# A hybrid encoder trunk on one core: four 512-frame blocks by seven products, the 32 new rows apart in fp32 column groups, a raw weight tile in another ring, loads ahead of frame pieces

## The chip, the cores and the metric

The kernel runs on one core of one Trainium2 chip. The metric is the device time of one execution in microseconds (us).

## The reference, cut to what matters

2048 frames of a new stream (x_prompt) and 32 frames of a running one (x_sample) pass one layer. Everything is fp32. Cut:

```python
def layer(h, p, conv_hist, pool_hist, pos, g_mix, w_in, conv_w, conv_b, pool_w, pool_scale,
          w_out, g_ple, w_ple_gate, w_ple):
    hn = rmsnorm(h, g_mix)
    proj = hn @ w_in                                # 1024 -> 6 kinds of 512
    hA, bA, cA, zA, vB, zB = jnp.split(proj, ...)
    yA, new_conv = short_conv_mixer(hA, bA, cA, zA, conv_hist, conv_w, conv_b)   # b*conv3(c*h)*silu(za)
    yB, new_pool = pooling_mixer(vB, zB, pool_hist, pos, pool_w, pool_scale)     # windows 2/4/8/16
    h = h + jnp.concatenate([yA, yB], axis=-1) @ w_out
    gate = jax.nn.sigmoid(rmsnorm(h, g_ple) @ w_ple_gate)
    h = h + (p @ w_ple) * gate
    return h, new_conv, new_pool
# then a last rmsnorm; the last 2 conv inputs and 15 pooling inputs of each stream are returned too
```

## The kernel before

Every large product is made of fp32r matmuls. An operand is split into a high part (a cast on ScalarE, `copy`) and a low part (a difference on VectorE), `split` (L79); three matmuls, high x high, high x low and low x high, stand for one (`FINE`, L160). Two blocks of frames and two halves of the depth make a 2 x 2 block product, and this is done by seven block products instead of eight: sums and differences of operand quarters ("11", "12", "21", "22", "S1" to "S4", "T1" to "T4") are prepared by VectorE; three PSUM banks X, Y, Z collect them. One block product is four depth steps x three matmuls = 12 matmuls.

**Input stage** (`with ExitStack() as s1`, L344). The 2080 rows are five blocks of NB = 416 frames; `GROUPS` (L26) puts them into two groups of two blocks and a third with the fifth block alone, whose last 32 columns are the new rows. For each group a loop over j = 0..3 (a "unit") makes 128 output channels of each of the six kinds. The frames are the moving operand (`B`), the weights the stationary one (`make` in `pair_weights`, which loads raw 512 KB tiles through SP into the `raws` ring and splits them). The first unit (`plain`) multiplies without the seven-product form, while `second_block` prepares the frame parts; the other units of the first two groups run `seven` (L1005), three pairs of kinds of 7 x 12 matmuls each. Between the steps of a pair `aside()` runs a part of side work at a set pace: in the first group, `next_columns` prepares the second group's frame parts (transposes on TensorE, sums on VectorE, to memory `p_d`, from which `load_group` fetches them); in the second group, `last_block` normalizes and turns the fifth block by way of memory (`x4_d`, `b_d`) and `turn_p` prepares the layer's embedding input (`pp_d`). After c and h, `mix` (L841) multiplies the pooled frames by pool_w: three matmuls for each block and unit. The third group's units are `plain` again, 6 x 24 matmuls each; meanwhile `early_sums` prepares the sum parts of w_out, and `early_embedding` the weights of the embedding.

**Transition.** Three embedding tiles (EARLY, L107) run between the third group and the output stage.

**Output stage** (from L1370). Eight pairs of 128-row tiles, `seven` (L220) with y as the stationary operand and w_out's parts as the moving one, 512 wide; a pair's seven products are 84 matmuls (L170, L175). The 32 new rows go through `plain` (L289) with `packed` (L278), whose stationary tiles are 64 and 32 wide. The results, h, go to memory.

**Embedding and gate.** Eleven embedding tiles, p @ w_ple, 12 matmuls each; the gate weights' parts are made at the same time; two late tiles (LATE) and the new rows' gate product follow; then eight gate pairs, `seven` again. The last pair makes its own embedding (`last_pair`).

**Start.** `first_tile` normalizes three 128-row tiles of x and one 64-row tile (`short0`: 32 rows each of blocks 0 and 1) and turns them on TensorE. `fill` (L390) adds transposes of the identity. Before them `gm` (L388), a product with a row of ones in plain fp32, spreads g_mix over the partitions.

**Order.** Each engine runs its instructions in order. The order in the program is laid out at build time, except where `keep_in_program_order` fixes it. SP issues most loads and the y stores, POOL the stores of frame parts. Pools are rings: a tile's load waits until the last reader of the tile that had its place is done.

Of the kernel before, what the change touches and what calls it, by code (L numbers as in the profile page):

```python
# [24 lines left out]
NB = 416  # L25
GROUPS = [[0, 1], [2, 3], [4]]  # L26
# [3 lines left out]
EARLY = 3  # L30
# [4 lines left out]
def trunk(ctx, tc, x_p, x_s, c_conv, c_pool, p_p, p_s, g_mix, w_in, conv_w, conv_b, pool_w,  # L35
# [12 lines left out]
    x4_d = tc.dram_tile([4, P, D], F32, name="x4_d")  # L48
# [49 lines left out]

    tiles = [(i * P, P) for i in range(SEQ // P)] + [(SEQ, DEC)]
# [14 lines left out]

    def load_pps(t, i, queue):
# [12 lines left out]
    def embed(todo, wp, ring, queue=nc.sync, loads=nc.sync):  # L128
# [4 lines left out]
        got = {}  # L133
# [26 lines left out]
    FINE = (0, 0), (0, 1), (1, 0)  # L160

# [15 lines left out]

    def weight_sums(W, k, top, bot):

        b11, b12, b21, b22 = top[:, :NH], top[:, NH:], bot[:, :NH], bot[:, NH:]
        for q, t, x, y in (("T1", b11, b12, b11), ("T3", b12, b22, b12), ("T2", b22, b22, b11), ("T4", b21, b21, b22)):
            nc.vector.tensor_tensor(t, x, y, op=ALU.subtract)
            split(W[q][0][:, k], W[q][1][:, k], t)

    def frame_parts(cmb, tmp, name, a11, a12, a21, a22):
# [10 lines left out]
        def comb(q, x, y, op):  # L199
            t = tmp.tile([P, KH, P], F32, tag="s", name=f"{name}_f{q}")  # L200
            nc.vector.tensor_tensor(t, x, y, op=op)
            return t

        s1 = comb("S1", a21, a22, ALU.add)
        put("11", a11)
        s2 = comb("S2", s1, a11, ALU.subtract)
        put("S2", s2)
        put("S1", s1)
        put("S3", comb("S3", a11, a21, ALU.subtract))

        def more(i):
            if i == 0:
                return put("12", a12)
            if i == 1:
                return put("S4", comb("S4", a12, s2, ALU.subtract))
            return put("22", a22)
# [92 lines left out]
    def halves(t):  # L309

        return [t[:, c * KH * NH:(c + 1) * KH * NH].rearrange("p (k n) -> p k n", k=KH) for c in range(3)]
# [4 lines left out]
    def sums_slots(name):  # L316
        a, b = halves(slot(f"{name}_a")), halves(slot(f"{name}_b"))
        t4 = seventh(f"{name}_T4").rearrange("p (h k n) -> p h k n", h=2, k=KH)
        return dict(T1=a[:2], T2=(a[2], b[0]), T3=b[1:], T4=(t4[:, 0], t4[:, 1]))
# [4 lines left out]
    def load_y(i, m):  # L324
        a = []
        for half in range(2):
            t = ring4(ya, f"y_{i}_{half}").rearrange("p (k t) -> p k t", k=KH)
# [3 lines left out]

    def load_top(k, t):
        nc.sync.dma_start(t[:, k % 2 * NH:k % 2 * NH + NH], w_out[k * P:(k + 1) * P, :NH])

    def load_bottom(k, t):
        return nc.sync.dma_start(t, w_out[(KH + k) * P:(KH + k + 1) * P])
# [7 lines left out]
    with ExitStack() as s1:  # L344
        pool = lambda name, bufs: s1.enter_context(tc.tile_pool(name=name, bufs=bufs))
        wr = pool("wr", 7)
        raws = pool("raws", 4)
        acts.append(ctx.enter_context(tc.tile_pool(name="acts", bufs=3, side="right")))
        frames_in = ExitStack()
        xin = frames_in.enter_context(tc.tile_pool(name="xin", bufs=5, side="right"))  # L350
        big = pool("big", 1)
        wk = pool("wk", 3)
# [13 lines left out]
        def ftile(name):  # L366
            return wk.tile([P, KH, P], F32, tag="f", bufs=4, name=name)
# [8 lines left out]
        halo_u = one.tile([P, 4, 2], F32, name="halo_u")  # L376
        halo_v = one.tile([P, 4, 15], F32, name="halo_v")
        nc.gpsimd.memset(halo_u, 0.0)
        nc.gpsimd.memset(halo_v, 0.0)


        gm_row = wk.tile([P, 2, 2 * NB], F32, tag="pp", bufs=1, name="gm_row").rearrange("p h n -> p (h n)")[:1, :D]
# [12 lines left out]
        short_bank = bank("pt0_3")  # L395
        fill(7, short_bank)
# [4 lines left out]
        def x_rows(tb, c):  # L401
            r = tb * NB + c * P
            if c < 3:
                return x_p[r:r + P]
            return x_p[r:r + DEC] if tb < 4 else x_s

        def x_load(name, rows):

            t, at = ring4(xin, f"xt_{name}"), 0
            for src in rows:  # L410
                m = src.shape[0]
                nc.sync.dma_start(t[at:at + m], src)
                at += m
            return t, at, f"x{name}"
# [5 lines left out]

        def x_tile(name, rows):
            return x_stat(x_load(name, rows))
# [15 lines left out]
        def columns_in(g, c):  # L438

            a, b = GROUPS[g]  # L440
            if c < 3:
                return [x_load(f"{tb}_{c}", [x_rows(tb, c)]) for tb in (a, b)]
            return [x_load(f"{a}_3", [x_rows(a, 3), x_rows(b, 3)])]

        def four(xs, tag):

            for half in range(2):
                if len(xs) == 2:
                    yield [turn(x, half, f"pt_{tag}_{i}_{half}", later=True) for i, x in enumerate(xs)]
                else:  # L450
                    t = turn(xs[0], half, f"pt_{tag}_{half}", later=True)
                    yield [t[:, :, :DEC], t[:, :, DEC:2 * DEC]]

        def frame_sums(xs, tag, dst):
# [9 lines left out]
            n = P if len(xs) == 2 else DEC  # L464
            f12, f1, f21 = (ftile(f"{c}_{tag}")[:, :, :n] for c in ("f12", "f1", "f21"))
# [5 lines left out]
            dst("11", p11, n)  # L471
            yield
            dst("T1", f1, n)
# [5 lines left out]
            dst("21", p21, n)  # L479
            yield  # L480
            dst("22", p22, n)
            yield
            dst("T2", f1, n)
# [1314 lines left out]
```

## Time and profile before

| | us |
|---|---|
| median of 3 runs | 922.1 |
| lowest, highest | 921.87, 922.18 |
| span of the profiled execution | 920.4 |
| TensorE busy in it | 907.0 |
| VectorE busy | 723.2 |
| ScalarE busy | 482.7 |
| GpSimd busy | 159.3 |

The profile shows one execution. PE is TensorE's matmuls, PEld its weight loads (they run beside matmuls), DVE VectorE, ACT ScalarE, POOL GpSimd, SP the queue that issues most loads. A line such as "L175 PE MATMUL x_o<-wo_b,y_S 128*128 128x512 f32 x128 | 35.7, 391" is a group of 128 matmuls of line 175 that write x_o from wo_b and y_S, 128 rows deep and 128 columns of stationary tile, 512 columns moving: busy time, mean ns of one. In a timeline the first figure is the start, the second the busy time, both in us, and a bracket names what ended the idle time before. A row of a table by stage begins with the stage's bounds and its length, then has for PE, PEld, DVE, ACT and POOL the busy time and the number of instructions, then the granted clock (1.00 is full), the DMA share and GB/s.

### The profile page before, as it was taken

Reading aid. Unit: us, or ns where it says so; the run is one execution under the profiler, and the core shown is the slowest. Engines: PE = TensorE matmul, PEld = TensorE weight load, DVE = VectorE, ACT = ScalarE, POOL = GpSimd, SP = SyncE. Lnnn points to the kernel's source line nnn. Section 1 sums busy time; section 2 is a strip of 40 time slices with the busy share of each in tenths; the row PEclk is TensorE's granted clock in tenths of the full one; section 3 lists DMA queues with packets and bytes.
Section 4 is the critical chain, followed back from the end, with each engine's and each line's share of the span. In section 5 each row is a group of like instructions: output and inputs, shape, how many; then the busy total and the mean of one; then the engine's idle time right before and its main releaser. Section 6 shows DMA issues by size and latency. Waiting matters only on the chain.

```text
span 920.4 us, 13201 instructions
## 1 busy us (share of the span) xinstructions
PE 907.0 (99%) x4529; PEld 824.7 (90%) x4529; DVE 723.2 (79%) x1236; ACT 482.7 (52%) x894; POOL 159.3 (17%) x307
## 2 busy tenths in 40 slices
PE   8999999999999999999999999999999999999996
PEld 6999999999999999999999988888878878888885
DVE  6996898999576989795777579666558658889885
ACT  6744565654345555453444365444436855555554
POOL 2111222121000342310000111111113301111113
PEclk9999999999999999999999999999999999999999
DMA  8357687898945789738885468865767974576554
GB/s 247 100 141 220 170 245 230 244 282 285 416 137 172 235 231 221 231 115 303 245 243 178 146 234 278 266 218 183 237 228 230 357 262 140 206 242 231 190 201 176
DMA packets 138447, 205.12 MB, mean 223 GB/s; under 512 B 13116, under 2 KB 101724, under 8 KB 137101
## 3 DMA queue, kind: packets, MB, share of 16 engines
q1 hardware_dynamic: 117773, 139.41, 47.9%
q0 software_dynamic: 17872, 59.45, 19.6%
q10 hardware_dynamic: 2736, 5.44, 1.6%
q8 instruction: 35, 0.57, 0.3%
q14 instruction: 31, 0.25, 0.1%
HBM read 136.60 MB, written 67.64 MB: 222 GB/s over the span
## 4 chain that ended last, share of the span: by engine, by line
PE 78%; DVE 6%; DMA 3%; issue 1%; ACT 1%; POOL 0%; POOLq 0%; DVEq 0%
PE x_o L175 9%; PE x_g L175 9%; PE x_zab L593 5%; PE z_g L175 5%; PE x_zbv L593 5%; PE e L107 4%; PE z_o L175 4%; PE x_ch L593 4%; PE z_zab L593 3%; PE z_zbv L593 2%; PE z_ch L593 2%; PE y_g L175 2%; PE y_o L175 2%; PE za L593 2%; PE b L593 2%; PE h L593 1%
## 5 line engine op out<-in xcount | busy, mean ns | idle before, releaser
L80 ACT CAST y_S<-y_fS 128x512 fp32r<-128x512 f32 x32 | 19.5, 622 | 36.8 <-PE x_o L175 19.0
L175 PE MATMUL x_g<-wg_b,g_S 128*128 128x512 f32 x128 | 35.7, 390 | 0.0
L175 PE MATMUL x_o<-wo_b,y_S 128*128 128x512 f32 x128 | 35.7, 391 | 0.0
L593 PE MATMUL x_zab<-B,w_zab_S 128*128 128x416 f32 x168 | 34.2, 352 | 0.2 <-ACT V L989 0.2
L593 PE MATMUL z_zab<-B,w_zab_S 128*128 128x416 f32 x168 | 34.3, 352 | 0.0
L593 PE MATMUL x_zbv<-B,w_zbv_S 128*128 128x416 f32 x168 | 34.2, 352 | 0.0
L593 PE MATMUL z_ch<-B,w_ch_S 128*128 128x416 f32 x168 | 34.1, 352 | 0.0
L593 PE MATMUL x_ch<-B,w_ch_S 128*128 128x416 f32 x168 | 34.0, 351 | 0.0
L593 PE MATMUL z_zbv<-B,w_zbv_S 128*128 128x416 f32 x168 | 34.0, 351 | 0.0
L107 PE MATMUL e<-wq,pps 128*128 128x512 f32 x144 | 33.1, 390 | 0.0
L593 PEld LDWEIGHTS x_zab<-B,w_zab_S 128*128 128x128 f32 x168 | 31.3, 188 | 0.8 <-ACT V L989 0.5
L107 PEld LDWEIGHTS e<-wq,pps 128*128 128x128 f32 x144 | 27.0, 188 | 5.6
L593 PEld LDWEIGHTS x_ch<-B,w_ch_S 128*128 128x128 f32 x168 | 31.4, 188 | 0.3
L593 PEld LDWEIGHTS z_zbv<-B,w_zbv_S 128*128 128x128 f32 x168 | 31.4, 188 | 0.3
L593 PEld LDWEIGHTS z_ch<-B,w_ch_S 128*128 128x128 f32 x168 | 31.4, 188 | 0.3
L593 PEld LDWEIGHTS z_zab<-B,w_zab_S 128*128 128x128 f32 x168 | 31.4, 188 | 0.3
L593 PEld LDWEIGHTS x_zbv<-B,w_zbv_S 128*128 128x128 f32 x168 | 31.3, 188 | 0.4
L1343 DVE TENSOR_TENSOR c_o<-x_o,x 128x512 f32<-128x512 f32 x14 | 9.7, 691 | 26.4 <-PE x_o L175 26.4
L1566 DVE SCALAR_TENSOR_TENSOR h<-h,rstd_f,g_bc 128x1024 f32<-128x1024 f32 (+1 forms) x15 | 19.3, 1284 | 14.0 <-POOL rstd_f L76 14.0
L72 POOL TENSOR_SCALAR ms_f<-ssq_f 128x1 f32<-128x1 f32 (+1 forms) x15 | 6.6, 441 | 128.7 <-ACT junk L93 128.5
L175 PEld LDWEIGHTS x_o<-wo_b,y_S 128*128 128x128 f32 x128 | 24.0, 188 | 5.2 <-DVE c_o L1343 0.3
L175 PEld LDWEIGHTS x_g<-wg_b,g_S 128*128 128x128 f32 x128 | 24.0, 188 | 5.0
(591 smaller groups left out, 2688.5 us busy)
## 6 DMA issues: line engine op xcount, KB each, us to landing
y<-y_d SPq DMA_DIRECT2D x16, 512.0 KB, 6.7
x<-in_x_prompt_dram SPq DMA_DIRECT2D x16, 512.0 KB, 4.3
h_d<-x SPq DMA_DIRECT2D x16, 512.0 KB, 3.8
h<-h_d SPq DMA_DIRECT2D x16, 512.0 KB, 3.7
xt<-in_x_prompt_dram SPq DMA_DIRECT2D x15, 512.0 KB, 7.2
e<-e_d SPq DMA_DIRECT2D x15, 512.0 KB, 6.3
out_dram<-h POOLq DMA_DIRECT2D x14, 512.0 KB, 3.0
p_dT<-T POOLq DMA_DIRECT2D x12, 512.0 KB, 6.0
```

The source lines that it names most:

```text
L72: nc.gpsimd.tensor_scalar(ms[:n], ssq[:n], scalar1=1.0 / D, scalar2=EPS, op0=ALU.mult, op1=ALU.add)
L80: ins = nc.scalar.copy(hi, src)
L107: nc.tensor.matmul(ps, pps[:, a, k], wp[k][b][:, cs], start=k + q == 0, stop=k == 1 and q == 2)
L175: nc.tensor.matmul(ps[:n], lhs[:, k, a, :n], w[b][:, k], start=start and k + q == 0, stop=k == KH - 1 and q == 2, skip_group_check=True)
L593: nc.tensor.matmul(ps[:, :NB], lhs[:, k, x], b[:, k, y], start=start and k + q == 0, stop=stop and k == KH - 1 and q == 2, skip_group_chec ...
L1343: add = lambda o, a, b: nc.vector.tensor_tensor(o, a, b, op=ALU.add)
L1566: nc.vector.scalar_tensor_tensor(h[:n], h[:n], rf[:n], g_bc[:n], op0=ALU.mult, op1=ALU.mult)
```

## The change

NB becomes 512: four blocks, two groups, and no third group. `last_block`, `x4_d`, `b_d` and the code for a block with old and new frames in it go. The 32 new rows are projected in the second group, as side work after `turn_p`: `new_frames` turns them once, loads w_in in 24 raw tiles of 128 x 1024 and multiplies each by four fp32 matmuls, without splitting; four groups of 32 PSUM partitions of one bank take four quarters of the columns. VectorE turns the results back, and the mixers of the new rows run on small tiles there.

```diff
-NB = 416
-GROUPS = [[0, 1], [2, 3], [4]]
+NB = 512
+GROUPS = [[0, 1], [2, 3]]
...
-EARLY = 3
+EARLY = 7
 LATE = 2
```

```diff
+        def new_frames():
+            x = x_stat(x_load("new", x_s), True)
+            yield
+            normal(x)
+            xt, n, _ = x
+            pt = tbank("pt_new")
+            for k in range(KC):
+                nc.tensor.transpose(pt[:, k * n:k * n + n], xt[:n, k * P:k * P + P], ident[:n, :n])
+            xs = ftile("xs")[:, :2].rearrange("p a (k n) -> p (a k) n", n=DEC)
+            nc.scalar.copy(xs, pt[:, :KC * DEC].rearrange("p (k n) -> p k n", n=DEC))
+            order = [(q, k) for q in range(3) for k in range(KC)]
+            def load(i):
+                q, k = order[i]
+                t = ring4(xin, f"wn_{q}_{k}")
+                nc.sync.dma_start(t, w_in[k * P:k * P + P, q * D:q * D + D])
+                return t
+            loaded = [load(0), load(1)]
+            yield
+            out = []
+            for i, (q, k) in enumerate(order):
+                if k == 0:
+                    ps = tbank(f"new_{q}")
+                t = loaded.pop(0).rearrange("p (kind j g c) -> p g kind j c", kind=2, j=4, g=4)
+                for g in range(4):
+                    nc.tensor.matmul(ps[g * DEC:g * DEC + DEC, :NB // 2].rearrange("p (kind j c) -> p kind j c", kind=2, j=4),
+                                     xs[:, k], t[:, g], start=k == 0, stop=k == KC - 1, skip_group_check=True)
+                if i + 2 < len(order):
+                    loaded.append(load(i + 2))
+                if k == KC - 1:
+                    o = ftile(f"new_{q}")[:, :2].rearrange("p a b -> p (a b)")
+                    nc.vector.transpose(o, ps[:, :NB // 2])
...
+                yield
...
+            pm = tbank("pm_new")
+            for j in range(4):
...
+                pool_means(j, v[:, j], HV, DEC, lambda: p, turn_of, False)
+                nc.tensor.matmul(pm[:, j * DEC:j * DEC + DEC], pwn[:, j], p, start=True, stop=True, skip_group_check=True)
```

The rings change with the wider blocks: `xin` 5 to 4, `raws` 4 to 3, `wr` 7 to 6; the pooled frames' ring `pps` also takes the second raw tile of the pair zb and v. Each unit loads its own 128 x 128 part of pool_w; pooling and conv go block by block, and the mixes stand at other steps. The next columns' x loads are issued before the last frame pieces of a column, on GpSimd's queue.

```diff
-                rb = raw_weight(kb, j, f"{name}b", ring)
+                rb = raw_weight(kb, j, f"{name}b", ring_b)
...
-                make = pair_weights(self.gi, ka, kb, self.j, name, ring, s_ring)
+                make = pair_weights(self.gi, ka, kb, self.j, name, ring, s_ring, pool_ring if ka == "zb" else ring)
...
-                    if i == 8 and after is not None:
-                        load_ahead(1, after)
+                    if i == 10 and after is not None:
+                        ahead[after] = columns_in(1, after, nc.gpsimd)
...
-                        aside = at_pace(chain(last_block(), turn_p()), 3, 5)
+                    aside = at_pace(chain(turn_p(), new_frames()), 1, 1)
```

At the start a fourth full tile takes the place of the 64-row one, and the first products of zb and v are cut into 384 and 128 columns.

```diff
-            if c < 3:
-                fill((2, 3, 2)[c], short_bank)
+            if c < 2:
+                fill((2, 20)[c], fill_bank)
...
+            early = slice(0, 3 * P), slice(3 * P, NB)
+            spans = [[(kind, early[0]) for kind in ("zb", "v")] + [(kind, early[1]) for kind in ("zb", "v")] + [("c", slice(0, NB))]]
```

The parts of w_out, which were made in the third group, are now made around seven embedding tiles and within the first output pair; the embedding's frames from the third tile on, and its results, lie in the places of T4 and of a frame slot.

```diff
+        with tc.issue_after(last_raw):
+            nc.sync.dma_start(g_bc, g_fin.partition_broadcast(P))
+            wp = early_weights()
+            early_pps = [load_pps(qa.tile([P, 2, 2, P], F32R, tag="q", name=f"pps_{i}"), i, nc.sync) for i in range(2)]
+            lo, hi = first_y = load_y(0, 2 * P, xh)
+            tops, _ = rows_of_weight(ya, "wo_t", w_out, 0)
+        weight_slot(W, "wo", *PLACES[0])
+        more = prep_h(0)
+        weight_parts(W, tops, None, "11", "T1")
...
+        for c in range(EARLY):
+            run(c)
+        first_x = [load_rows(xh, "x", b, x_p) for b in range(2)]
+        bots, loaded = rows_of_weight(cmb, "wo_b", w_out, 1)
...
+        weight_parts(W, tops, bots, "T2")
...
+        LATER = {1: later("T3"), 2: place_last, 3: later("22", 1), 4: later("T4", 2)}
```

Before the gate stage the weight parts come one kind after the other, the top rows' first; the two late embedding tiles join the others (nine tiles now follow the output stage), and the new rows' gate product moves between the gate pairs.

```diff
+        tops, _ = rows_of_weight(ya, "wg_t", g_d, 0)
+        weight_slot(W, "wg", *PLACES[0])
+        weight_parts(W, tops, None, "11", "T1")
         S = {}
-        A = short("gl", turned(NT - 1), n, ya)
-        for step in prep_g(0).values():
-            step()
+        steps = prep_g(0)
+        steps[2]()
+        bots, _ = rows_of_weight(xh, "wg_b", g_d, 1)
+        for names in PLACES[1:]:
+            weight_slot(W, "wg", *names)
+            weight_parts(W, tops, bots, *names)
+        weight_seventh(W, "wg")
+        weight_parts(W, tops, bots, "T4")
+        steps[3]()
         hn_queue[0] = nc.sync
-        for c in range(len(rest_e) - LATE, len(rest_e)):
-            run(c)
...
+            if i in (2, 4):
+                next(short_steps)
```

More of the change, by code (lines that the diff above doesn't have):

```diff
@@ L943, in plain @@
+                self.mix(1)
+                next(second)
+                nc.vector.tensor_copy(U[:, :HU], halo_u[:, :, j])
                 wh = weights("h", j, f"h{tag}")
@@ L1332, in half_of @@
+        early = ExitStack()
+        wpe = early.enter_context(tc.tile_pool(name="wpe", bufs=4, side="right", reuse_waits="tile"))
         def half_of(x, at, n=P):
```

814 lines of the change are left out of this document (352 added, 462 removed).

## The prediction

> **What bounds the kernel now.** I read the head of the page first (busy time by engine, the 40 slices, the chain that ended last), then TensorE's waits, then a table of busy time by stage, then TensorE's timeline for the pace of each kind of matmul.
>
> ```profile
> span 920.4 us, 13201 instructions
> PE 907.0 (99%) x4529; PEld 824.7 (90%) x4529; DVE 723.2 (79%) x1236; ACT 482.7 (52%) x894; POOL 159.3 (17%) x307
> PEclk9999999999999999999999999999999999999999
> PE 78%; DVE 6%; DMA 3%; issue 1%; ACT 1%; POOL 0%; POOLq 0%; DVEq 0%
> ```
>
> TensorE is busy 99% of the span at the full granted clock, and 78% of the chain runs through it. Its waits:
>
> ```profile
> PE gm L388 <- DVE V L826: 2.3, 1, 2.3
> PE pt_g L433 <- DVE 11_1_1_1643 L83: 1.1, 1, 1.1
> PE zb L621 <- DVE B L667: 0.8, 1, 0.8
> PE pt L433 <- DVE xt L641: 0.7, 1, 0.7
> ```
>
> They are a few us in all. So the time is the number of matmuls times the pace of each, plus waits that the change adds. The stages (start and first unit; three units of the first group; the second group; the fifth block):
>
> ```profile
> 0.00:76.00 76.00, 71.74 (x377) 66.77 (x378) 64.01 (x120) 44.24 (x88) 12.82 (x55) 1.00 0.60 168
> 76.00:230.40 154.40, 153.15 (x831) 150.06 (x831) 140.66 (x240) 85.51 (x161) 35.02 (x48) 1.00 0.78 241
> 230.40:426.00 195.60, 195.42 (x1033) 192.94 (x1033) 156.33 (x267) 97.23 (x181) 36.44 (x60) 1.00 0.73 229
> 426.00:539.00 113.00, 112.58 (x594) 109.98 (x594) 79.24 (x181) 50.21 (x100) 10.19 (x20) 1.00 0.66 204
> ```
>
> VectorE (third pair of figures) is at 140.66 of 154.40 us in the first group: the next limit, if the change added work to it there.
>
> **The products, 416 wide to 512 wide.** A busy time overlaps its neighbour's, so a pace is read from start to start.
>
> ```profile
> 342.15 2.43 PE L593 MATMUL x_zbv<-B_T,w_zbv 128*128 128x416 f32 x12
> 344.42 0.93 PE L593 MATMUL x_ch<-B,w_ch 128*128 128x416 f32 x4
> ...
> 585.88:604.92 19.04, 19.04 (x85) 15.77 (x84) 11.67 (x18) 8.00 (x13) 2.90 (x7) 1.00 0.74 242
> ```
>
> Twelve 416-column matmuls start in 344.42 - 342.15 = 2.27 us, 0.1892 each. An output pair is 7 products of 12 matmuls 512 wide, in 19.04 us: 0.2267 each. From the code: the first unit is 2 blocks x 6 kinds x 24 matmuls = 288, the other seven units of the two groups 7 x 3 x 84 = 1764, and the fifth block 4 x 144 = 576, which goes. Before, 2628 x 0.1892 = 497.2; after, 2052 x 0.2267 = 465.2. That is -32.0; cutting 16 of them into 384 + 128 columns costs by the straight line through the two paces (0.39 ns a column, 25 ns fixed) 0.4, so **-31.6**. The twelve small products of the fifth block leave the pooling maps at 48 x 0.2267 instead of 60 x 0.1892: **-0.5**.
>
> The fifth block's stage ran 113.00 us for 576 + 12 matmuls at 0.1892 and four small transposes at 0.10 (below): 111.7. The 1.3 us of waits in it go too: **-1.3**.
>
> **Transposes and small matmuls.** 128 transposes of x 128 wide take the place of 96, and 24 of the 64-wide ones go.
>
> ```profile
> 114.60 1.04 PE L433 MATMUL pt_g<-ident,xt 128*128 128x128 f32 x8
> 115.39 2.51 PE L593 MATMUL x_zab<-B,w_zab_S 128*128 128x416 f32 x12
> ```
>
> Eight take 0.79 us, 0.10 each, and so about do the narrow ones: 32 x 0.10 - 24 x 0.10 = +0.8. The new rows' eight narrow transposes and four pooling maps add about 1.2 by the same pace and two passes each; two state transposes fewer take 0.2. Together **+1.8**.
>
> **The new rows, the disputed term.** 24 raw tiles of w_in, each with four matmuls of fp32 words: the 32 rows stationary (128x32, in columns 0, 32, 64 or 96 of the array), 256 columns moving. The trace has one matmul in plain fp32, and products with narrow stationary tiles:
>
> ```profile
> 2.26 3.75 PE L388 MATMUL gm<-gm_row,ones 1*128 1x512 f32 x4 [2.26 <-DVE V L826]
> 5.93 1.75 PE L393 MATMUL pt<-ident 128*128 128x128 f32 x7
> 7.48 1.28 PE L433 MATMUL pt<-ident,xt 128*128 128x128 f32 x5
> ...
> 681.08 1.08 PE L284 MATMUL x_ol<-wo_c,yl 128*64 128x512 f32 x4
> 682.00 1.09 PE L287 MATMUL x_ol<-wo_c,yl 128*32 128x512 f32 x4
> 682.93 1.07 PE L284 MATMUL z_ol<-wo_a,yl 128*64 128x512 f32 x4
> ```
>
> Two gm instructions are four records: an fp32 matmul is two passes. 5.93 - 2.26 = 3.67 us is 0.917 a pass of 512 columns, at a start-up rate at which a 128-wide transpose took 0.22 (1.55 for seven), half the pace of the 0.10 above. At full rate and 256 columns a pass is 0.917 / 4 = 0.229, a matmul 0.459. The bounds: all 96 one after the other, 96 x 0.459 = 44.0; the four of a tile side by side, 24 x 0.459 = 11.0. The trace shows no two matmuls in different column groups. I take the middle: TensorE starts matmuls in order; a matmul's second pass needs the same column group as its first and so waits for it, and the next group's first pass runs beside that second pass. Each matmul then costs one pass: 96 x 0.229 = **+22.0**.
>
> The rows 681.08 to 682.93 also price the switch of tile shape: four matmuls 64 wide, then 32 wide, take 0.92 and 0.93 us, 0.23 each, as at 128. I put the switches at nothing. The Trainium skill says otherwise: TensorEngine Tiling (Array Packing), section Key Properties, has the TensorE drain whenever the tiling mode changes. These rows don't show it, though they stay within one accumulation. If each of the 19 places where new-row matmuls stand between 128-wide products drained twice, at duration less pace of a 512 matmul (0.39 - 0.23, from the row x_o of the last fence), it would be 19 x 2 x 0.16 = +6.1.
>
> Their loads (512 KB each, 12.6 MB in about two units) go through SP behind the weight loads and y stores. In program order the products between a slot's release and its tile's use, at 0.2267 each, come to 5.8 to 14.5 us; rows below give 4.3 to 6.3 for 512 KB. At nothing; a late one costs its lateness, TensorE being in order (0 to +5). VectorE does less per column in wider blocks and loses the fifth block's bounce; adding up its operations at their rows' durations I get some 52 us in a first-group unit of 61. No new bound.
>
> **Start.**
>
> ```profile
> 12.74 1.38 PE L433 MATMUL pt<-ident,xt 128*128 128x128 f32 x8 [0.68 <-DVE xt L641]
> 14.26 0.93 PE L650 MATMUL pt<-ident,xt 64*128 64x64 f32 x8
> 16.02 1.75 PE L621 MATMUL zb<-B,w_firstzb 128*128 128x416 f32 x8 [0.83 <-DVE B L667]
> ```
>
> The first product started 1.76 us after the transposes of a 64-row tile. In its place stands a fourth full tile: four times the bytes to load and eight wide transposes (1.5 us here, the array not yet warm), with seventeen more warm-up transposes between, under VectorE's scalings. **+1.0**, between 0 and +2.5.
>
> **Between the stages.** Three embedding tiles stood between group and output stage; now seven do.
>
> ```profile
> 538.99 8.60 PE L107 MATMUL e<-wp,pps 128*128 128x512 f32 x36
> 539.84 2.74 DVE L1423 TENSOR_TENSOR wo_c<-wo_q,wo_c 128x512 fp32r<-128x512 f32 x4
> 541.83 2.20 SPq L336 DMA_DIRECT2D wo_q<-in_w_out_dram  x4
> ...
> 707.60:751.00 43.40, 43.40 (x201) 33.17 (x200) 26.38 (x43) 29.45 (x57) 10.28 (x19) 1.00 0.91 324
> ...
> x<-in_x_prompt_dram SPq DMA_DIRECT2D x16, 512.0 KB, 4.3
> e<-e_d SPq DMA_DIRECT2D x15, 512.0 KB, 6.3
> ...
> L1343 DVE TENSOR_TENSOR c_o<-x_o,x 128x512 f32<-128x512 f32 x14 | 9.7, 691 | 26.4 <-PE x_o L175 26.4
> L175 PE MATMUL x_o<-wo_b,y_S 128*128 128x512 f32 x128 | 35.7, 391 | 0.0
> ```
>
> The total of embedding matmuls is the same; the seven tiles are cover, 84 x 0.2267 = 19.0 us, for work that lay under the fifth block's 113 us: the weight parts of w_out, 12 differences and 20 low parts after the top rows, 32 x 0.69 = 22 us of VectorE. The third to seventh embedding tiles' frames can only load when the group's last product has freed T4's place: 5.8 us of two tiles' matmuls against 4.3 to 6.3: **+1.0** (0 to +1.5). The bottom rows are issued behind the last y stores, some 4 us after the group's end, and behind 4 MB, which take 13 us at the 324 GB/s of the busiest stage below, so they land about 13 us after it. T2's eight operations are done at 18.5, asked for at 19.0 + 2 x 2.72 = 24.4; T3, 21 and the frames' 12 (16 operations more) at 29.5, asked for from 27.2 on as each is reached. **+1.0**, between 0 and +6.
>
> Before the gate stage its weight parts now come without the two late embedding tiles and the short product in front: 31 VectorE operations, 19 to 21 us, under nine tiles' 24.5. What stays open is the last hop: transposes, ScalarE's high part, VectorE's low part, 0.7 us each: **+1.5**, between 0 and +3. The other reordered loads and the shorter rings I put at nothing, 0 to +3.
>
> **Sum.** -31.6 - 0.5 - 1.3 + 1.8 + 22.0 + 1.0 + 1.0 + 1.0 + 1.5 = -5.1. Against the execution's own 920.4 that is 915.3; the median of the runs (922.1) lies 1.7 above that span, so **917 us**.
>
> **Rivals.**
>
> *Side by side.* The four column groups run at once, passes and all: 11.0 instead of 22.0, so 906. For it: each group has its own columns and its own outputs. Against: no row here shows two matmuls at once. The Trainium skill, TensorE: Matmul & The Clock Gate, Part 3 (Packing small matmuls), states this mechanism: tiles in different groups start some 4 ns apart and the whole takes one matmul's time; no run before the change shows it. It does not speak of matmuls in two passes.
>
> *One after the other, the slower side.* Nothing overlaps, because four groups need four streams of moving data: 44.0, so 917 + 22 = 939. For it: every narrow product in the trace costs what a full one does (0.23). It decides by itself: from 27.1 us of new rows on (22.0 + 5.1) the gain of the wide products is eaten up.
>
> *The array empties at each change of tile shape,* before and after the new-row matmuls of each of the 19 places: +6.1, so 923. Against it, the 0.23 above.
>
> *Output weights late.* T3 and 21 reach VectorE after the bottom rows have landed 6 us later than reckoned, and the first pair's fourth and fifth products wait that long: +5 beyond what I took, 922. For it: a few us of slack only, and DMA at 204 to 241 GB/s in all four stages. Against: 19 us of cover, and the 2.20 us that four such loads took to issue at 541.83.
>
> **Chances.** Half overlapped 0.42 (own range 911 to 923); side by side 0.19; one after the other 0.18; emptied array 0.08; late weights 0.13. About 0.2% (1.8 us, 920.3 to 923.9) is what a measurement of this kernel can tell from no change. Faster: 0.19 + most of the first (0.28) + a little of the last two (0.04) = 0.51. Same: 0.09 of the first + 0.05 of the last two = 0.14. Slower: 0.18 + 0.05 of the first, where unseen waits add up, + 0.12 of the last two = 0.35. The range runs from the side-by-side case, 905, to the serial one, 939.
>
> **What would show it.** A product of twelve should start to start take 2.72 us in all eight units, and the fifth block's 113 us be gone. The new rows' records should be 192, and the time from a tile's first record to the next 128-wide product 0.9 us (right), 0.46 (side by side), 1.8 (serial); a gap of over 0.1 ahead of each group would be a drain. TensorE's waits should name DMA for e and VectorE for x_o or y_o by no more than 1 to 2 us each. A wait of several us on a wn load, or VectorE full in a first-group unit, would make the prediction wrong.

## The result, and the profile after

The changed kernel takes 962.67 us (median of 4 runs, 960.25 to 964.99), the kernel before 922.08 on the same chip (921.87 to 922.18). The ratio is 1.0448, 95% interval 1.0425 to 1.0471: slower by some 40 us. The prediction was 917, from 905 to 939, so the time lies outside its range.

The head of the page of the changed kernel: span, busy time by engine, and the granted clock in 40 slices.

```profile
span 959.7 us, 12177 instructions
PE 909.6 (95%) x4186; PEld 728.2 (76%) x4186; DVE 697.4 (73%) x1146; ACT 457.7 (48%) x826; POOL 142.9 (15%) x282
PEclk9999999999997899999999999999999989999999
```

TensorE runs 343 matmuls fewer (4186 for 4529) and is busy 2.6 us longer. No engine is full; TensorE stands idle for 50 us instead of 13. The full clock of before is gone in some slices. TensorE's longest waits:

```profile
PE z_ch L612 <- DVE w_ch_S L84: 15.2, 1, 15.2
PE pth L1448 <- ACT ho L1446: 3.2, 1, 3.2
PE e L109 <- DMA pps<-pp_d: 2.9, 1, 2.9
PE y_o L185 <- ACT y L81: 2.7, 1, 2.7
...
PE z_o L185 <- DVE c_o L1255: 1.7, 1, 1.7
PE pt_new L1084 <- DVE xt_new L452: 1.5, 1, 1.5
```

The list of before had one row over 1.1 us. Where the time went, by stage: the table by windows, of the kernel before and then of the changed one. The rows are the input stage, the embedding tiles ahead of the output stage (three, then seven), the output stage, and the rest.

```profile
0.00:538.99 538.99, 532.89 (x2832) 519.74 (x2832) 440.23 (x806) 277.19 (x530) 94.47 (x183) 1.00 0.71 218
538.99:547.42 8.43, 8.43 (x37) 6.65 (x36) 5.08 (x8) 5.63 (x11) 0.00 (x0) 1.00 0.54 176
547.42:707.51 160.09, 160.09 (x705) 129.99 (x705) 109.90 (x171) 74.97 (x126) 26.52 (x52) 1.00 0.71 238
707.51:920.40 212.89, 205.56 (x959) 168.34 (x957) 167.96 (x252) 124.88 (x228) 38.34 (x73) 0.99 0.65 224
```

```profile
0.00:553.65 553.65, 527.89 (x2488) 421.38 (x2489) 398.09 (x686) 245.39 (x446) 80.33 (x158) 0.98 0.62 196
553.65:575.49 21.84, 19.78 (x86) 15.70 (x85) 15.80 (x26) 13.64 (x26) 3.23 (x6) 1.00 0.92 315
575.49:746.29 170.80, 163.39 (x705) 130.49 (x704) 114.00 (x181) 76.26 (x131) 26.45 (x52) 0.99 0.73 236
746.29:959.70 213.41, 198.55 (x911) 160.60 (x909) 169.55 (x256) 122.38 (x223) 32.92 (x66) 0.98 0.63 205
```

Input stage +14.7, output stage +10.7, embedding and gate (second and fourth rows together, since four tiles moved from one to the other) +13.9: 39.3 us in all, in every stage, though the work was changed mostly in the first.

**The 15.2 us.** They lie at the start of the second group. TensorE's, VectorE's, SP's and GpSimd's timelines of the changed kernel there, and the group's loads in the view of the DMA (queue totals between 262 and 312 us, then one load with its time from issue to landing; last, the queue totals between 280 and 290 us alone):

```profile
313.71 4.63 PE L612 MATMUL z_ch<-B,w_ch_S 128*128 128x512 f32 x10 [15.22 <-DVE w_ch_S L84]
```

```profile
311.64 0.69 DVE L588 TENSOR_TENSOR s_zab<-raw_zab_0b 128x512 f32<-128x512 f32 x1 [28.04 <-DMA raw_zab_0b<-in_w_in_dram]
...
312.98 0.69 DVE L84 TENSOR_TENSOR w_ch_S<-s_ch,w_ch_S 128x512 fp32r<-128x512 f32 x1
```

```profile
265.75 1.29 POOL L535 DMA_DIRECT2D B<-p_d  x2
...
268.84 1.37 SPq L548 DMA_DIRECT2D raw_zab_0b<-in_w_in_dram  x1
```

```profile
q0 software_dynamic: 1296, 15.73, 77.0%
q1 hardware_dynamic: 5147, 3.15, 21.7%
...
raw_zab_0b<-in_w_in_dram SPq DMA_DIRECT2D x1, 512.0 KB, 42.7
```

```profile
q0 software_dynamic: 280, 4.06, 96.4%
q1 hardware_dynamic: 279, 0.14, 4.7%
```

It begins with that load: a 512 KB weight tile was issued 3 us after the first frame pieces and took 42.7 us to land. VectorE reached the sum that reads it and stood there for 28 us; the low part w_ch_S, for which everything had been there, was behind it in VectorE's order, and TensorE waited for that. Before, the same tile was issued just ahead of the frame pieces, as the two queues' timelines of before show:

```profile
217.76 0.38 SPq L529 DMA_DIRECT2D raw_zab_0b<-in_w_in_dram  x1
...
219.56 1.10 POOL L517 DMA_DIRECT2D B<-p_d  x2 [8.88 <-PE y_zab L593]
```

VectorE read it there at 232.1 without waiting for it, so it had landed within 14.3 us.

The queue totals say why it took so long: GpSimd's queue (q0) moved 15.73 MB in 1296 packets, 12 KB each, SP's (q1) 3.15 MB in 5147, 0.6 KB each. The Trainium skill, DMA: Bandwidth & Descriptors, section Queues, rings and completion order, states that each DMA engine goes round the queues packet by packet. By that rule SP's queue gets 0.6 of every 12.6 KB; 5% of the some 400 GB/s moved here (18.9 MB in 50 us) is 20 GB/s, an estimate of 52 us for the two tiles of the pair, 1 MB, if the rule's packets are those that the trace counts. The measured 42.7 agrees in size, and the trace agrees packet by packet while the pieces run: between 280 and 290 us the two queues moved 280 and 279 packets, and SP's got 0.14 of 4.2 MB, 14 GB/s. Not all of the 42.7 went at that pace: between 270 and 300 us SP's queue moved 0.39 MB, and between 300 and 310, as the pieces ended, 1.12 MB.

**The clock after a wait.** Rows of the table by windows of the changed kernel; the first figure after the last count in brackets is the granted clock.

```profile
313.70:318.20 4.50, 4.49 (x11) 3.52 (x12) 3.84 (x6) 3.90 (x8) 0.00 (x0) 0.50 0.02 4
...
408.00:410.00 2.00, 2.00 (x18) 0.80 (x20) 0.22 (x1) 0.00 (x0) 0.00 (x0) 0.50 1.00 253
587.70:591.50 3.80, 3.80 (x10) 2.94 (x11) 3.80 (x7) 3.80 (x8) 0.00 (x0) 0.55 0.02 4
760.20:763.00 2.80, 2.75 (x12) 2.31 (x13) 1.61 (x3) 1.26 (x3) 0.00 (x0) 1.00 1.01 407
```

After the waits that ended at 313.71 (15.2 us), 406.3 (1.5) and 587.7 (2.7) the array runs at half clock for 3.4 to 4.4 us, and the eleven matmuls of the first row take 4.5 us where 2.5 are due: each such wait costs about 2 us more than it shows. The wait of 3.2 that ended at 776.47 is followed by half clock until 782, 2.6 us lost. After the wait that ended at 760.2 (2.9) the clock stays full.

**The new rows.** TensorE's timeline of the changed kernel, two of the 19 places:

```profile
418.36 0.64 PE L1103 MATMUL new<-wn,xs 128*32 128x256 f32 x8
418.93 3.02 PE L612 MATMUL x_zab<-B_T,w_zab 128*128 128x512 f32 x12
421.88 1.07 PE L1103 MATMUL new<-wn,xs 128*32 128x256 f32 x16
422.88 1.45 PE L612 MATMUL x_zbv<-B,w_zbv 128*128 128x512 f32 x5
```

One tile (8 records) takes 0.57 us from its first start to the next product's, two tiles 1.00: a tile costs 0.43, the four matmuls' two passes side by side. But the twelve products between two places take 421.88 - 418.93 = 2.95 instead of 2.72. So a place costs 0.57 - 0.43 = 0.14 inside and 0.23 around it, 0.37 beside its tiles. All of it is 24 x 0.43 + 19 x 0.37 = 17.4 us.

What the 0.37 comes from is not settled. The new rows' matmuls differ from the products around them in two ways: a narrower stationary tile, and plain fp32 in two passes. Two rows of the kernel before, ahead of and behind the narrow products of its output stage, and three of the changed kernel, where the new rows' pooling maps (plain fp32, two passes of 32 columns, a full 128x128 tile) stand between products:

```profile
678.36 2.88 PE L175 MATMUL x_o<-wo_T,y 128*128 128x512 f32 x12
688.45 2.90 PE L175 MATMUL x_o<-wo_c,y 128*128 128x512 f32 x12
```

```profile
484.26 0.30 PE L1141 MATMUL pm_new<-new_y,pw_new 128*128 128x32 f32 x2
484.40 2.33 PE L612 MATMUL z_zab<-B,w_zab_S 128*128 128x512 f32 x9
486.57 2.89 PE L612 MATMUL x_zab<-B,w_zab_S 128*128 128x512 f32 x12
```

Before, the twelve products ahead of the narrow ones took their 2.72 us (to 681.08), and the 32 products with stationary tiles of 64 and 32 columns in turn took 7.37 us to 688.45, where 32 x 0.2267 = 7.25 are due: nine changes of shape cost 0.12, and 0.02 more in the twelve products behind them (to 691.19). In the changed kernel one pooling map takes 0.14 and the nine products behind it 2.17 where 2.04 are due, 0.27 in all without any change of shape. So a part of the 0.37, at least, goes with plain fp32 between fp32r products; no run separates the two.

### The profile page after: what moved, and what is told of

Same layout as the page of the kernel before. It is cut to its first block, busy times and chain, and to the rows that moved or that the text cites. A ratio compares the mean times of both kernels' runs of the same rounds, so it can differ in the third digit from the quotient of the medians.

```text
span 959.7 us, 12177 instructions
## 1 busy us (share of the span) xinstructions
PE 909.6 (95%) x4186; PEld 728.2 (76%) x4186; DVE 697.4 (73%) x1146; ACT 457.7 (48%) x826; POOL 142.9 (15%) x282
## 3 DMA queue, kind: packets, MB, share of 16 engines
q0 software_dynamic: 17200, 59.32, 18.9%
## 5 line engine op out<-in xcount | busy, mean ns | idle before, releaser
L612 PE MATMUL z_ch<-B,w_ch_S 128*128 128x512 f32 x168 | 43.4, 407 | 16.5 <-DVE w_ch_S L84 15.2
L185 PE MATMUL z_o<-wo,y_S 128*128 128x512 f32 x192 | 47.6, 391 | 2.4 <-DVE c_o L1255 1.7
L185 PE MATMUL x_o<-wo_T,y_S 128*128 128x512 f32 x192 | 47.7, 398 | 0.9 <-ACT c_o L1260 0.9
L185 PE MATMUL z_g<-wg,g_S 128*128 128x512 f32 x192 | 47.6, 392 | 0.0
L185 PE MATMUL x_g<-wg_T,g_S 128*128 128x512 f32 x192 | 46.6, 390 | 0.0
L612 PE MATMUL z_zab<-B,w_zab_S 128*128 128x512 f32 x168 | 42.2, 396 | 0.0
L612 PE MATMUL x_ch<-B,w_ch_S 128*128 128x512 f32 x168 | 42.0, 392 | 0.0
L612 PE MATMUL x_zab<-B,w_zab_S 128*128 128x512 f32 x168 | 41.1, 391 | 0.0
L612 PE MATMUL z_zbv<-B,w_zbv_S 128*128 128x512 f32 x168 | 40.7, 391 | 0.0
L612 PE MATMUL x_zbv<-B,w_zbv_S 128*128 128x512 f32 x168 | 40.7, 391 | 0.0
L612 PEld LDWEIGHTS x_zbv<-B,w_zbv_S 128*128 128x128 f32 x168 | 31.6, 189 | 7.4 <-issue 0.8
L612 PEld LDWEIGHTS z_zab<-B,w_zab_S 128*128 128x128 f32 x168 | 31.6, 190 | 7.3 <-issue 0.8
```

What stands on the lines that cost most here:

```text
L185: nc.tensor.matmul(ps[:n], lhs[:, k, a, :n], w[b][:, k], start=start and k + q == 0, stop=k == KH - 1 and q == 2, skip_group_check=True)
L612: nc.tensor.matmul(ps, lhs[:, k, x], b[:, k, y], start=start and k + q == 0, stop=stop and k == KH - 1 and q == 2, skip_group_check=True)
```

## The experiments

All change the kernel after the change. Spans are those of the profiled execution, against 959.7; ratios are to the kernel before on the same chip.

### The weight tile that lands late: order on VectorE, or the load

The first experiment keeps the two sums of za and b in their place in the program, behind w_ch_S.

```diff
-                nc.vector.tensor_tensor(s_t, a21, a22, op=ALU.add)
-                sub(a21, a11, a21)
+                in_turn = tc.keep_in_program_order if (gi, ka) == (1, "za") else lambda ins: ins
+                in_turn(nc.vector.tensor_tensor(s_t, a21, a22, op=ALU.add))
+                in_turn(sub(a21, a11, a21))
```

> Only VectorE's order changes: the two sums of the raw za and b tiles in the second group's first unit stand behind that unit's zb/v and c/h work instead of ahead of w_ch_S. Theory (a wait on VectorE's queue: TensorE stood 15.2 us for w_ch_S because VectorE sat at the sums until raw_zab_0b landed at 311.6): the 15.2 us and the 2.2 us at half clock behind them go, a span of about 942 (959.7 - 17.4). Rival (the transfers themselves are too slow for the unit: TensorE would next wait for the same tile or for a frame piece): the wait moves to x_zab or z_zbv and the span stays above 950.

Measured: span 952.7, ratio 1.038 (1.035 to 1.041). The wait of 15.2 is replaced by a shorter one, for the pair's own products, as the rival had it:

```profile
PE x_zab L613 <- ACT w_zab L81: 6.3, 1, 6.3
```

So the order on VectorE made 9 of the 15 us, and the landing itself the rest: with the sums out of the way TensorE gets as far as the first product that needs the late pair, whose first tile, raw_zab_0a, landed at 311.56.

The second leaves VectorE alone and issues the pair's raw tiles through GpSimd's queue, behind two of the seven frame pieces and ahead of the other five.

```diff
-            for q in NAMES:
+            for q in NAMES[:2]:
                 nc.gpsimd.dma_start(B[q].bitcast(F32), p_d[q])
+            for kind, r, queue in (("zb", raw_ring, nc.sync), ("v", pool_ring, nc.sync), ("za", raw_ring, nc.gpsimd), ("b", raw_ring, nc.gpsimd)):
+                t = raw_weight(kind, 0, f"ahead{kind}", r, queue)
+                loaded_raw[kind, 0] = t
+            with tc.issue_after(raw_loads[-1].ins):
+                for q in NAMES[2:]:
+                    nc.gpsimd.dma_start(B[q].bitcast(F32), p_d[q])
...
```

> VectorE's order stays; the raw za and b tiles of the same unit are loaded through GpSimd's queue behind the first two of the seven 2 MB frame pieces and ahead of the other five. Theory (the load took 42.7 us because it shared the DMA engines with 14.7 MB of frame pieces in large packets): it lands before 285, VectorE does not stand, span about 942 to 945; a frame piece up to 3 us later may cost up to 3. Rival (the tile is late because its place in the smaller ring comes free late): the issue time stays near 268.8 and so does the 15 us wait, span about 960.

Measured: span 945.8, ratio 1.0298 (1.0268 to 1.0328). The wait is gone; 13.9 us of span come back. A new, smaller wait shows that the pieces behind the tiles now come late in their turn:

```profile
PE x_zbv L620 <- DMA B<-p_dT: 2.1, 1, 2.1
```

The two tiles were issued no earlier than in the changed kernel (269.12 and 270.04, against 268.24 and 268.84), but landed in 15.4 and 16.6 us. So the shorter ring's late place, the rival, is not what the 15 us hang on: the cause is the load's way beside the frame pieces, and in-order VectorE made it worse. The run changes the tiles' queue and their order against the pieces together; which of the two does it is not separated.

### The new rows in one column group

```diff
-                    nc.tensor.matmul(ps[g * DEC:g * DEC + DEC, :NB // 2].rearrange("p (kind j c) -> p kind j c", kind=2, j=4),
+                    nc.tensor.matmul(ps[(0 if k else g) * DEC:(0 if k else g) * DEC + DEC, :NB // 2].rearrange("p (kind j c) -> p kind j c", kind=2, j=4),
```

> The new rows' matmuls of all four groups from the second depth step on write the same 32 columns of the array, so the new rows' results are not the reference's; 84 of 96 are concerned. Side by side (the rows of the changed kernel: four passes start 7 ns apart, a tile takes 0.43): each of 21 tiles then takes eight passes one after the other, 8 x 0.213 = 1.70: +26.7 us of TensorE in 400 to 480. Had the groups not run together before, or if only the alternation mattered, it would be +0 to +5.

Measured: span 988.0, 28.3 longer. TensorE's timeline:

```profile
422.72 1.91 PE L1103 MATMUL new<-wn,xs 128*32 128x256 f32 x8
424.56 2.79 PE L612 MATMUL x_zab<-B_T,w_zab 128*128 128x512 f32 x11
```

Eight passes in one column group take 1.84 us one after the other, the place's own 0.14 included (so 0.21 each), against 0.57 in four groups. The groups do run side by side, and it is their being different groups that does it.

### The start of the output stage

SP's queue, ScalarE's and TensorE's timelines of the changed kernel:

```profile
556.41 11.28 SPq L371 DMA_DIRECT2D x<-in_x_prompt_dram  x2
567.81 2.08 SPq L1325 DMA_DIRECT2D wo_b<-in_w_out_dram  x4
...
584.95 2.18 ACT L197 CAST wo<-wo_b 128x512 fp32r<-128x512 f32 x4 [0.88 <-DMA e_d<-eouts]
...
587.70 1.06 PE L185 MATMUL y_o<-wo,y 128*128 128x512 f32 x2 [2.65 <-ACT y L81]
```

The bottom rows of w_out were issued 14 us after the group's end (553.65), behind two x loads that held SP for 11.28 us. The next experiment puts them ahead of the x loads.

```diff
-        first_x = [load_rows(xh, "x", b, x_p) for b in range(2)]
         bots, loaded = rows_of_weight(cmb, "wo_b", w_out, 1)
+        with tc.issue_after(loaded.ins):
+            first_x = [load_rows(xh, "x", b, x_p) for b in range(2)]
```

> The four loads of w_out's bottom rows go ahead of the first pair's two x loads on SP; nothing else moves. Theory (the first output pair waits for weight parts because SP held the bottom rows back from 556.4 to 567.8 behind x loads that had no place yet): the rows are issued about 8 to 11 us earlier and the waits of the first pair (about 6.5 us from 580 to 606, with their half-clock stretch) shrink by 4 to 6: span about 954 to 956. Rival (VectorE's own 32 operations are the bound): the waits stay, span about 959.

Measured: span 960.1, ratio 1.0469 (1.0436 to 1.0501): no gain. The first of the bottom rows was issued 10 us sooner, but SP now stood at these four loads themselves for 12.30 us, and VectorE was through its eight sums of top and bottom rows by 578.0 instead of 581.4. They were not what ended last: ScalarE's cast of part 21 waits for something else, and the wait y_o grows to 4.0:

```profile
557.51 12.30 SPq L1325 DMA_DIRECT2D wo_b<-in_w_out_dram  x4
...
585.76 2.18 ACT L197 CAST wo<-wo_b 128x512 fp32r<-128x512 f32 x4 [3.97 <-DMA e_d<-eouts]
```

The embedding results lie in the place of the weight parts 21 and 22 until their stores are done. So the sixth and seventh result got tiles of their own, on top of the edit above.

```diff
+            if i >= 5:
+                return ring4(xh if i == 5 else ya, f"eout_{i}")
             return space[:, i * D:i * D + D]
```

> As the run with the bottom rows first, and the sixth and seventh embedding results lie in other tiles than the place of w_out's 21 and 22 parts. There ScalarE's cast for 21 waited 4.0 us for the last stores out of that place (they landed at 585.7). Theory (two limits in a row: first the bottom rows, then the shared place): the cast starts at about 582, TensorE's wait for y_o falls from 4.0 to under 1.5 us and its half-clock stretch goes: span 4 to 6 below the 960.1 of that run, about 955. Rival (VectorE's chain of weight parts is the bound by itself): the wait stays over 2.5, span 959 or more.

Measured: span 954.2, ratio 1.0384 (1.0354 to 1.0414), 5.9 less than without it. The wait y_o is gone; one of 2.4 for x takes part of its gain. Against the changed kernel the two edits together bring 5.5 us; the second was not tried without the first.

### The start of the gate stage

GpSimd's, ScalarE's and TensorE's timelines of the changed kernel:

```profile
769.82 0.54 POOL L371 DMA_DIRECT2D hn<-h_d  x1 [5.73 <-issue]
...
775.80 0.62 ACT L1446 COPY ho<-hn 128x512 f32<-128x512 f32 x1 [2.23 <-DMA hn<-h_d]
...
776.47 2.12 PE L1448 MATMUL pth<-ident,ho 128*128 128x128 f32 x8 [3.21 <-ACT ho L1446]
```

The transposes of the first gate pair wait for a load of h that was issued only at 769.82. One experiment puts two embedding tiles back behind the first pair's preparation, as before the change; the other gives that load a place of its own (the one T4's parts take later).

```diff
...
-        for c in range(len(rest_e)):
+        for c in range(len(rest_e) - LATE):
...
+        for c in range(len(rest_e) - LATE, len(rest_e)):
+            run(c)
```

> The last two embedding tiles stand behind the first gate pair's preparation again, as before the change. Theory (without them nothing covers the hop load of h, ScalarE, transposes, high and low parts: 4.5 us of waits and some 2 us at half clock at 776 to 782): span about 953 to 955. Rival (the load of h is late itself, held by the gate weights' places, so two tiles of cover of 4.9 us only move the wait): span 957 to 960.

Measured: span 960.4, ratio 1.0461 (1.043 to 1.0491): the same as the change. The load was issued at 772.26, later again, and the wait pth is still 2.8, so it was not cover behind the load that lacked.

```diff
...
-        steps[2]()
         bots, _ = rows_of_weight(xh, "wg_b", g_d, 1)
+        first_hn.append(weight_seventh(W, "wg").bitcast(F32)[:, :D])
+        nc.gpsimd.dma_start(first_hn[0], h_d[:P])
...
-        weight_seventh(W, "wg")
+        steps[2]()
+        steps[3]()
         weight_parts(W, tops, bots, "T4")
-
-        steps[3]()
```

> The first gate pair's tile of h is loaded into the still empty place of T4, and its other tile is turned after the weight parts instead of ahead of the last output products on VectorE. Theory (the load at 769.8 waited for a place that the gate weights held, and the turn at 738.8 kept VectorE from c_o): TensorE's waits for pth (3.2 + 0.8, and 2 to 3 at half clock) and for c_o at 740 (1.7) go: span 951 to 953. Rival (VectorE's 31 weight operations and the frame parts themselves end too late): the wait moves to g or g_S, span 956 to 960.

Measured: span 955.9, ratio 1.0433 (1.0369 to 1.0497). The load was issued at 751.07 instead of 769.82, and the wait pth is gone from the list; another, e <- ACT wg_T, 2.0, has come. The wait for c_o, which was to go too, grew from 1.7 to 2.4. That the load lacked a place is shown; by time alone this run is not to be told from the change, since the intervals overlap.

### The mends together

The two edits for the raw tiles, the two for the output stage and the place for h, in one kernel:

> All at once: the raw za and b tiles loaded between the frame pieces and summed later, the bottom rows first, the embedding results apart, the gate's h in T4's place. If the waits are separate their gains add: 13.9 + 2 + 5 + 8 = 29, a span of about 931 and a time within 1.5% of the kernel before. If one wait hides another, less: 937 to 943.

Measured: span 940.1, ratio 1.0246 (1.0216 to 1.0276): the second of the two cases, the gains do not simply add. Waits of 2.2 to 2.6 remain for x_zbv, e, x_o and z_o. Three of those and the new rows' transposes were taken up next:

```diff
-            for q in NAMES[:2]:
+            for q in NAMES[:4]:
...
+            for _ in range(2):
+                yield
             xt, n, _ = x
             pt = tbank("pt_new")
...
-        LATER = {1: later("T3"), 2: place_last, 3: later("22", 1), 4: later("T4", 2)}
+        LATER = {1: later("T3"), 2: place_last, 3: later("22", 1), 4: later(2), 5: later("T4")}
...
-            nc.vector.transpose(t, t)
+            ins = nc.vector.transpose(t, t)
+            if i == 1:
+                tc.keep_in_program_order(ins)
```

> On top of the four mends of e8: the raw za/b loads of the second group's first unit go behind four of the seven frame pieces on GpSimd's queue instead of two, the gate's h tile is turned where the program has it in VectorE's order (behind the weight parts) and not earlier, the new rows' eight transposes stand two steps of side work later, and the sums for T4 one output step later. Theory (each remaining wait has a named operation standing ahead of it in an in-order queue, and costs its idle time plus about 2 us of half clock where it is over 1.5 us): the span of e8, 940.1, loses the wait x_zbv <- DMA B (2.2 + 2), c_o (2.6 + 1.5), pt_new (1.4) and part of e <- wg_T (0 to 4), so 929, between 926 and 932, mean clock above 0.994. Rival (the queues are full in these stretches, and a load or a turn put later makes something else late by as much): waits of 2 to 3 us under other names in the same places, 935 to 941.

Measured: span 930.9, ratio 1.0147 (1.013 to 1.0164), within the theory's 926 to 932. Of the four waits named, those for c_o and wg_T are gone, x_zbv is down from 2.2 to 1.3, and pt_new hardly moved (1.4 to 1.2). Its table by windows, in the order of the tables above:

```profile
0.00:536.06 536.06, 524.63 (x2488) 418.69 (x2489) 397.51 (x686) 245.72 (x446) 82.05 (x160) 1.00 0.64 203
536.06:558.00 21.94, 19.80 (x87) 15.70 (x85) 17.30 (x29) 13.62 (x26) 3.21 (x6) 1.00 0.90 317
558.00:724.42 166.42, 163.02 (x706) 130.52 (x705) 115.02 (x184) 77.56 (x135) 28.88 (x55) 0.99 0.77 244
724.42:930.90 206.48, 196.00 (x911) 158.91 (x909) 166.88 (x250) 121.72 (x220) 32.62 (x64) 0.99 0.63 210
```

The input stage is now 2.9 us shorter than before the change, the output stage 6.3 longer, embedding and gate 7.1 longer. In the second output pair TensorE still waits 2.3 us for VectorE, which works back to back from 556 to 582 us. A last run gives VectorE one embedding tile more of cover there, and puts the new rows' transposes later again:

```diff
-EARLY = 7
+EARLY = 8
...
-            for _ in range(2):
+            for _ in range(4):
```

> On top of the seven mends of e9: an eighth embedding tile ahead of the output stage (eight behind it), and the new rows' eight transposes four steps of side work later than in the change instead of two. Theory (in the first output pairs VectorE works back to back from 555 to 582 on the parts of w_out and y and is 2.3 us behind TensorE; one more tile, 12 x 0.2267 = 2.72 us, gives that cover): the wait x_o <- DVE y at 581 (2.4 with 1.2 of half clock) goes, and pt_new (1.4) with it, so a span of 926, between 924 and 929. Rival (the gate stage's parts then lack the cover that was given away, 2.7 us, where e9 waits 1.1 and 0.5): a wait of 2 to 4 us before the gate pairs, 930 to 933. In both the kernel stays slower than before, 920.

Measured: span 935.1, ratio 1.0189 (1.0153 to 1.0225). Both theory and rival fail. The gate stage got no longer wait, but the wait in the second pair stayed exactly as long, though VectorE now stood idle twice (1.50 and 1.89 us) ahead of it:

```profile
PE x_o L185 <- DVE y L84: 2.3, 1, 2.3
```

The 4.2 us more than the run before are in part other waits (e 3.0 for 2.1, the frame pieces 2.0 and 1.0 for 1.3), in part the half clock behind the wait in the second pair, which lasts to 592 here (0.50 from 585.95; 3.0 us lost, 1.5 in the run before). So what TensorE waits for in the second pair does not hang on cover ahead of the stage. The trace shows where the awaited operation stands: the high part of this y was cast by 575.9, and VectorE made the low part at 585.20, behind fifteen operations without a gap, eight of them for T4. That its place in VectorE's order is the cause was not tried. No version beat the kernel before.

## Why the prediction was wrong, step by step

- **Bound by TensorE, at full clock.** True of before, and the step from there failed: the sum took each term at full clock and each wait at its own length. After the change the waits set the time, and of the four single waits of over 2 us behind the start three (15.2, 3.2 and 2.7, not 2.9) are followed by some 2 us lost to half clock.
- **Products.** Right. Twelve take 2.72 us apart from the edges, and the fifth block is gone. That gain is in the time; it was covered up. The start, put at +1.0, came out close: the first product began at 16.64 instead of 16.02.
- **The new rows.** Put at 22.0 as half overlapped, they cost 17.4. Both sides of it were wrong: the four groups run side by side, passes too (10.3 for the 24 tiles, near the rival's 11.0), and going to the new rows' matmuls and back, put at nothing, costs 0.37 at each of the 19 places, 7.0 us, near the 6.1 of the emptied array. Of the two rules of the Trainium skill weighed in the prediction the first (TensorE: Matmul & The Clock Gate, Part 3) agrees with the measurement. The second (TensorEngine Tiling (Array Packing), Key Properties), a drain at each change of tiling mode, is not shown to be the cause, though the 6.1 reckoned from it has the right size: the trace does not tell the mode, the narrow fp32r products of before change shape at next to no cost, from and to 128-wide ones too, and plain fp32 costs 0.27 with a full tile.
- **"The other reordered loads and the shorter rings I put at nothing, 0 to +3."** This is the step that failed most. With the new rows at 17.4, the prediction's own terms for the input stage come to -13.2 (-31.6 - 0.5 - 1.3 + 1.8 + 17.4 + 1.0); it came out at +14.7. Of these 28 us 15.2 are the wait for the late weight tile and 2 the half clock after it; the wait for the new rows' transposes (1.5) and its half clock bring 3; the rest are waits of 1.5 us or less and some 4 us that I did not trace. The load experiments showed the first part: 13.9 us come back when that pair's loads alone are moved. I had reckoned VectorE's work in a unit and the slack of the new rows' loads, but not which load each reordered load now stands behind.
- **The output transition, +1.0 (0 to +6), and the late weights (+5).** The output stage grew by 10.7, of which 7.4 are idle time of TensorE (none before). The place was right, of the mechanism one half: the bottom rows were issued 10 us later than I had them, and still moving them ahead gained nothing by itself. Then a shared place held the parts, that of the embedding results until their stores are done, which the prediction did not look at (5.9 us on top of the first edit). The argument there from 204 to 241 GB/s in all four stages misreads its own table, where the first stage has 168; nothing in the sum hangs on it.
- **The gate transition, +1.5, and the embedding frames, +1.0.** Together 13.9 for embedding and gate. Again a place: the load of h waited for one that the gate's weight parts held. The hop of transposes and splits that I priced was there, behind it. Of the 13.9 only the load's wait (3.2, and 2.6 of half clock) was traced to a cause; the others, such as the 2.9 for the frames of e, were not tested one by one.
- **The rivals.** One after the other, the slower side, has the wrong mechanism: a single column group costs 28.3 more, and the kernel does not do that. None of the rivals was the late load: of the 0.35 for slower, only the unseen waits (0.05) were of the kind that decided.

## What to carry to other kernels

A change that reorders loads and shortens rings needs a ledger of its own: for each load, what stands ahead of it in its queue, which instruction frees its place, and what stands behind its first reader in that reader's engine. A small load that slips behind large transfers on another queue can land far later than it did (42.7 us here, within 14.3 before), and an in-order engine that reaches it early passes the wait on to work that had everything it needed. Where TensorE was at 99%, price each new wait of more than about 2 us with the half clock that can follow it.

## What the runs showed of the hardware

- Half clock came after short waits. In the changed kernel one of 2.7 us was followed by a row at 0.55, and one of 1.5 us, with eight 32-wide transposes right behind it, by rows at 0.75 and 0.50, while one of 2.9 us was followed by full clock. The Trainium skill, TensorE: Matmul & The Clock Gate, section HAM oscillation, gives idle gaps over some 3.4 us as the limit; these runs show it below that, and not by a fixed length of the wait alone.
- fp32 matmuls of two passes in four column groups interleave: 0.43 us for a tile's eight passes, 1.70 in one group (1.84 with the place's own 0.14).
- Going from 128-wide fp32r products to 32-wide plain fp32 matmuls and back costs 0.37 us each time beside those matmuls, most of it in the products on either side. With a full-width tile plain fp32 still costs 0.27, its two passes included, while nine changes between fp32r tiles 128, 64 and 32 wide cost 0.14 together.
